# Two-layer encoder on one core: convolution taps spread over the attention, half of their products on VectorE, GpSimd held until the first exponential, and softmax sums inverted before they are turned

## The chip, the cores and the metric

The kernel runs on one core of a Trainium2 chip. The metric is the device time of one execution in microseconds (us), median of several; lower is better. The engines are PE (TensorE, matrix products and transposes), DVE (VectorE), ACT (ScalarE), POOL (GpSimd) and SP (SyncE, which here only issues transfers). POOL also issues transfers, among them all that add into their destination.

## The reference

Two layers of latent attention beside a convolution module, then a gated feed-forward block with a short convolution, on 1024 tokens of width 1024. Cut to what matters here:

```python
for l in range(DEPTH):                       # 2
    h = _rmsnorm(x, g_mix[l]); p = h @ w_in[l]
    ...                                      # q, k, v of 8 heads from low-rank latents
    sc = q_nope @ k_nope.T + q_rope @ k_rope.T          # 1024 x 1024 per head
    y_attn = softmax(sc * scale) @ v
    a, gt = split(p[..., o3:]); u = a * sigmoid(gt)
    u = _dwconv(u, w_dw_conv[l], b_dw_conv[l])          # 31 taps, 512 channels, depthwise
    u = silu(_layernorm(u, g_conv_ln[l], b_conv_ln[l]))
    x = x + concatenate([y_attn, u]) @ w_o[l]
    ...                                      # gated feed-forward block, 2 x 2816 wide
return _rmsnorm(x, g_final)
```

## The kernel before

Everything lies with its channels on the 128 partitions and the 1024 tokens along the row, so the 512 convolution channels are four blocks `u[0]` to `u[3]` (in traces `gate`) with running sums `conv[0]` to `conv[3]`. Products are made in float32 with split operands (names ending in h and l). On PE, DVE, ACT and POOL the program's order is the order written by hand; the transfers of SP are ordered by the framework.

A layer has three stages: `project` (input projections, the near taps of the convolution on DVE), `attention`, and `feed` (output projection, normalizations, feed-forward block). In the profiled execution the attention of layer 0 lies about from 198 to 410 us and that of layer 1 from 1320 to 1530 us.

**The attention's steps.** `attention` walks over 64 pairs of a head and a tile of 128 queries. Step n holds, in this order: for odd n the product of probabilities and values of an earlier pair of tiles (`values`, `o`, line 1565), the transposes of tile n (`turn`, `t`, line 1539) with two copies out of PSUM into `pt` (ACT line 1541, DVE line 1542), the scores of tile n+2 (`s`, line 1516) with their row maximum on DVE (`mx`, line 1518), an exponential on ACT (`p`, line 1526), and last whatever stands in `agenda[n]`, a list of pieces of other work by step. A `values` reads both copies of two tiles, so a late `pt` on either engine stops PE. Two heads share a tile `yt`: `gather` adds the halves of a product into it.

**Row sums.** The exponential leaves row sums as columns `sums` (128 queries x 8 tiles). After a head's last `gather`, `sums` turns them on PE (`sr`, 8 x 128 in PSUM), inverts them on DVE (`rs`, line 1594), writes them to memory and reads them back spread over 64 partitions (`rb`). For every second head POOL multiplies `yt` by `rb` (line 1598) `Y_DELAY` steps later, and later still ACT casts the product (`ys_..h`, line 197) and POOL takes the difference (`ys_..l`, line 199). The last two heads use another way (`inverse`, `spread`).

**Late taps.** The taps that are left after `project` (`away`) are made during the attention by `tap_late`: a product of the shifted block and one column into `late` (line 1723, on POOL or DVE), and then the addition into `conv[j]`, for block 0 on POOL (line 1727), for the other blocks by an adding transfer that POOL issues (line 1729). Two adding transfers into the same block follow each other: the second is issued when the first has landed. The taps of the four blocks take turns, and the step of each comes from running costs (`LATE_COST`, `SIDE_TIME`); block 3 has 15 late taps, block 2 has 11, blocks 0 and 1 have 12 (11 in layer 1). A tap whose product is on DVE has it at the head of an agenda of an even step (steps 4 and 6 of each eight), and its transfer in the next step.

**The end of the attention.** From step 50 on POOL casts weights of the output projection (`wo`, line 850), ACT makes their second part (line 178) and POOL completes them by an adding transfer (line 179). At steps 60 to 62 `conv_total` adds the four blocks into `lns` on POOL (line 1735), and after step 64 `conv_split` casts it on ACT (line 1739) and takes the rest on DVE (line 1740).

Of the kernel before, what the change touches and what calls it, by code (L numbers as in the profile page):

```python
# [9 lines left out]
F32 = mybir.dt.float32  # L10
# [45 lines left out]
SECTION = {"kr": 7.3, "k": 2.72, "u": 4.08, "n": 4.08, "v": 2.72}  # L56
TAP = 1.28
FFN_BANKS = (2, 4)
SIDE_TIME = 57
TOTAL_TIME = 60  # L60
Y_DELAY = 5
Y_LAST = 4
WO_AT = 50
ROWS = (3, 4)
ROW_AT = {0: (6,), 1: (7,)}
# [1 line left out]
MANUAL = [E.PE, E.DVE, E.Activation, E.Pool]  # L67
LATE_COST = {"pool": 2.3, "both": 3.8, "vector": 0.9}
LATE_ADDED = 0
NEAR_TAPS = (12, 14, 16, 14)  # L70
NEAR_ORDER = (0, 1, 2, 3)
FAR_TOGETHER = 3
# [42 lines left out]
class Encoder:  # L115
# [125 lines left out]
    def turned(self, acc, name, parts, bank):  # L241
        out = []
        for s in parts:
            ps = bank(name + "t")
            for b in range(0, s.stop - s.start, 128):
                self.nc.tensor.transpose(ps[:, b:b + 128], acc[:, s.start + b:s.start + b + 128], self.ident)
            out.append(ps[:, 0:s.stop - s.start])
        return out
# [267 lines left out]
    def project(self, l, carry):  # L516
# [54 lines left out]
        def glu(j):  # L571
# [6 lines left out]
            todo = [t for t in range(KC) if t != PAD]  # L578
            taps.extend((j, t) for t in todo[:NEAR_TAPS[j]])
            taps.sort(key=lambda e: NEAR_ORDER.index(e[0]))  # L580
            away[j] = todo[NEAR_TAPS[j]:]
            far_at[j] = 0.0
# [250 lines left out]
    def layer(self, l, carry):  # L833
        with self.psum(f"mix{l}", ([f"w{i}" for i in range(3)], 1), 2):
            mixed = self.project(l, carry)
        with self.psum(f"attn{l}", 2, 2):
            casts, ready = {}, {}
            cast = lambda ms: [casts.update({m: self.wo_cast(l, m, 1)}) for m in ms]
            ahead = {WO_AT: lambda: cast(range(4)), WO_AT + 6: lambda: cast((4, 5)), 62: lambda: cast((6, 7))}
            for m, when in enumerate((55, 59, 60, 62)):  # L840
                ahead[when] = lambda m=m, f=ahead.get(when, lambda: None): (ready.update({(1, m): self.complete(*casts.pop(m))}), f())
            begun = {"x": {}, "po": {}}
            conv, ys = mixed[1], self.attention(l, *mixed, ahead, ready, begun)
        with self.psum(f"ffn{l}", 0, ([f"d{i}" for i in range(8)], 1)):
            return self.feed(l, conv, ys, ready, casts, begun["x"])()
# [43 lines left out]
    def wo_steps(self, l, conv, ys, w, casts, x, steps, put):  # L889
        nc, a, par = self.nc, self.a, self.par[l]  # L890
        left, right = HALVES
        casts, ps, acc, sq, rf, us = {(1, m): e for m, e in casts.items()}, {}, {}, {}, {}, []
# [11 lines left out]
        def turn(part, m):  # L904
            w[part, m] = self.complete(*casts.pop((part, m)))

        put(-3, 0, load_x)
        put(1, 6, self.last_pair)
        for m in range(4, 8):
            put(-1, 3, lambda m=m: turn(1, m))  # L910
        for m in range(8):
            put(m // 4, 5, lambda m=m: cast(0, m))
# [575 lines left out]
    def attention(self, l, u, conv, away, spill, keys, kvs, loaded, ahead, wo, begun):  # L1488
        nc = self.nc
# [3 lines left out]
        state, v = {}, []  # L1493

        def rows(tt):
            (kv, wv), ts = kvs, slice(tt * 128, (tt + 1) * 128)
            ps = self.bank(f"pv{l}_{tt}")
            for k in range(2):
                for s, (i, j) in enumerate(((0, 0), (0, 1), (1, 0))):
                    nc.tensor.matmul(ps, kv[k][i][:, ts], wv[j][:, k * 512:(k + 1) * 512],  # L1500
                                     start=(k == 0 and s == 0), stop=(k == 1 and s == 2))
            if tt % 2 == 0:
                v.append(self.blk(f"v{l}_{tt}", F32, (128, 2, 512)))
            (nc.vector.tensor_copy if tt % 2 else nc.scalar.copy)(out=v[tt // 2][:, tt % 2], in_=ps)
# [69 lines left out]
        def gather(h, gg, main, aux, n):  # L1574
            st = state[h]
            y, rb, po = st["y"], st["rb"], st["po"]
            qs = HALVES[gg]
            nc.scalar.copy(out=y[main, qs], in_=po[aux, :])
            nc.vector.tensor_tensor(out=y[main, qs], in0=po[main, :], in1=y[main, qs], op=ALU.add)
            if h < HEADS - 2:  # L1580
                if gg:
                    agenda[n + 1].append(lambda: sums(h, main, st, y, rb))
            elif n > total:
                divide(y[main, qs], main, h, gg)
            else:
                agenda[n + 1].append(lambda: divide(y[main, qs], main, h, gg))
                if h == last:
                    agenda[n + 1].append(lambda: finish(last, y, 0))

        def sums(h, main, st, y, rb):  # L1590
            pr = self.bank(f"sr{l}_{h}", (8, 128))
            nc.tensor.transpose(pr, st["sums"], self.ident)
            rs = self.cp.tile([8, 128], F32, name=f"rs{l}_{h}", tag="rs", bufs=2)
            nc.vector.reciprocal(out=rs, in_=pr)
            nc.sync.dma_start(out=sd[h].rearrange("(a b) -> a b", a=8), in_=rs)
            nc.sync.dma_start(out=rb[main, :], in_=sd[h:h + 1].partition_broadcast(64))
            if h % 2:
                agenda[h * 8 + 10 + Y_DELAY].append(lambda: nc.gpsimd.tensor_tensor(out=y, in0=y, in1=rb, op=ALU.mult))
                agenda[h * 8 + 10 + Y_DELAY + (Y_DELAY if h < 5 else Y_LAST)].append(
                    lambda: ys.append(self.split(y, f"ys{l}_{h}", on_pool=True)))  # L1600
# [29 lines left out]
        ys, inv, po = [], {}, begun["po"]  # L1630
        total = HEADS * 8
        agenda = defaultdict(list)
        late = [(j, away[j][i]) for i in range(max(map(len, away.values()))) for j in range(4) if i < len(away[j])]
        kinds = ["both" if j == LATE_ADDED else "vector" if i % 4 == 2 and i < len(late) - 6 else "pool" for i, (j, _) in enumerate(late)]
        costs, taken = [LATE_COST[kind] for kind in kinds], set()
        for i, (j, t) in enumerate(late):
            n, steps = int(SIDE_TIME * sum(costs[:i]) / sum(costs)), self.tap_late(l, j, t, u[j], conv[j], kinds[i])
            if kinds[i] == "vector":
                while n % 8 not in (4, 6) or n in taken:
                    n += 1  # L1640
                taken.add(n)
                agenda[n].insert(0, lambda steps=steps: next(steps))
                n += 1
                agenda[n].append(lambda steps=steps: next(steps, None))
            else:
                agenda[n].append(lambda steps=steps: (next(steps), next(steps, None)))
        for when, f in ahead.items():
            agenda[when].append(f)
        last = HEADS - 1
# [5 lines left out]
        self.last_pair = lambda: finish(last, state_y(), 1)  # L1655
        for i in range(1, 4):
            agenda[TOTAL_TIME + i - 1].append(lambda i=i: self.conv_total(l, conv, i))
        agenda[total].append(lambda: self.conv_split(l))
        for n in range(-2, total + 1):
            if n % 2 and n > 2:  # L1660
                values((n - 3) // 2, n)
# [8 lines left out]
            if n + 2 < total:  # L1670
                h, qt = divmod(n + 2, 8)
# [197 lines left out]
```

## Time and profile before

| | us |
|---|---|
| median of 3 runs | 2262.45 |
| the runs | 2262.25, 2262.45, 2269.5 |
| profiled execution, its own time | 2264.65 |
| span of the profiled execution, first to last instruction | 2262.9 |
| PE busy | 2231.8 |
| DVE busy | 1670.9 |
| ACT busy | 1233.4 |
| POOL busy | 729.8 |

Busy time says how long an engine had an instruction under way; PE is busy for 99% of the span, so what matters is the little time in which it waits, and the time in which its clock is lowered (the column PEclk of a table of stretches, 1.00 is the full clock). Rows of the timeline give the start in us, the duration, the engine, the line, the operation, output and inputs; in brackets the idle time of the engine before, and what ended it.

### The profile page before, as it was taken

The numbers are of one execution on the slowest core, as the hardware profiler recorded it, in microseconds if no ns is written. First come the engines' busy times: TensorE is split into PE (matmuls) and PEld (weight loads), VectorE is DVE, ScalarE is ACT, GpSimd is POOL, SyncE is SP. The second block draws the span as 40 slices with busy tenths as digits, with TensorE's granted clock in tenths as the row PEclk, the third lists the DMA queues.
The fourth block names the chain that finished last, engine by engine and source line by source line (L and its number), as shares of the span: only waits on it lengthen the run. The fifth ranks groups of instructions, "written<-read, shape, count | busy, mean of one in ns | idle before, by whom it ended". The sixth has DMA issues, their size and how long they took to land. (4 is left out here: it accounts for less than half of the span.)

```text
span 2262.9 us, 34450 instructions
## 1 busy us (share of the span) xinstructions
PE 2231.8 (99%) x12746; PEld 1790.5 (79%) x12746; DVE 1670.9 (74%) x2200; ACT 1233.4 (55%) x1885; POOL 729.8 (32%) x808
## 2 busy tenths in 40 slices
PE   9999999999999999999999999989999999999998
PEld 7887666787888888888888876667888888888887
DVE  6997877668877776776559778866787777768665
ACT  5444777446655555544533557764475555555444
POOL 1222676432333333001412235762323333320032
PEclk9999999999999999999999999999999999999999
DMA  6889998855899998935968999987669999988356
GB/s 187 164 176 275 188 205 180 205 168 122 216 279 299 274 301 204 336 103 142 211 136 167 194 270 198 191 182 188 162 141 235 277 299 277 298 205 308 103 127 167
DMA packets 201161, 472.85 MB, mean 209 GB/s; under 512 B 28353, under 2 KB 35617, under 8 KB 200993
## 3 DMA queue, kind: packets, MB, share of 16 engines
q0 software_dynamic: 102704, 220.91, 48.6%
q1 hardware_dynamic: 98000, 249.35, 33.3%
q8 instruction: 100, 1.64, 0.3%
q14 instruction: 69, 0.56, 0.1%
q10 hardware_dynamic: 288, 0.39, 0.0%
HBM read 306.14 MB, written 80.40 MB: 171 GB/s over the span
## 5 line engine op out<-in xcount | busy, mean ns | idle before, releaser
L1076 PE MATMUL p<-b,w 128*128 128x512 f32 x3552 | 808.0, 389 | 1.2 <-ACT zv L1087 1.1
L1076 PEld LDWEIGHTS p<-b,w 128*128 128x128 f32 x3552 | 665.8, 188 | 142.8 <-ACT zv L1087 2.2
L1264 PE MATMUL pd<-ab,wd 128*128 128x512 f32 (+1 forms) x1920 | 422.3, 381 | 0.0
L1264 PEld LDWEIGHTS pd<-ab,wd 128*128 128x128 f32 x1920 | 350.7, 188 | 69.5 <-DVE ab L1454 0.4
L179 POOL DMA_DIRECT2D w<-wu x96 | 84.2, 877 | 359.5 <-ACT w L178 323.0
L1518 DVE TENSOR_REDUCE mx<-s 128x1 f32<-128x1024 f32 x128 | 156.2, 1220 | 39.0 <-PE s L1516 31.2
L1526 ACT ACTIVATE p<-s,mx 128x1024 f32<-128x1024 f32 x128 | 143.0, 1117 | 60.0 <-DVE mx L1518 58.3
L1466 DVE SCALAR_TENSOR_TENSOR o<-zg,par,o 128x1023 f32<-128x1023 f32 x88 | 112.8, 1284 | 75.4 <-ACT o L1460 74.0
L179 POOL DMA_DIRECT2D w<-in_w_up x116 | 100.4, 866 | 201.2 <-ACT w L178 181.6
L1710 DVE SCALAR_TENSOR_TENSOR conv<-gate,par,conv 128x1009 f32<-128x1009 f32 (+7 forms) x112 | 142.3, 1274 | 3.6 <-ACT conv L575 1.0
L1565 PE MATMUL o<-pt,v 128*64 128x256 f32 x1024 | 128.1, 388 | 14.1 <-ACT pt L1541 9.4
L178 ACT ACTIVATE w<-w 128x512 fp32r<-128x512 f32 x212 | 133.5, 630 | 3.1
L1025 DVE TENSOR_TENSOR zg<-p,zg 128x512 f32<-128x512 f32 x88 | 60.6, 690 | 99.7 <-PE p L1076 92.9
L1452 ACT CAST ab<-ac 128x512 fp32r<-128x512 f32 x130 | 80.1, 617 | 98.5 <-DVE ac L1199 96.0
L850 POOL DMA_DIRECT2D wd<-in_w_down x44 | 32.6, 745 | 309.5 <-PE pd L1264 309.4
L1542 DVE COPY pt<-t 128x512 f32<-128x512 f32 x128 | 87.8, 686 | 56.5 <-PE t L1539 49.9
L1466 DVE SCALAR_TENSOR_TENSOR v<-zv,par,v 128x1023 f32<-128x1023 f32 x88 | 112.5, 1280 | 10.5 <-ACT v L1460 10.4
L1565 PEld LDWEIGHTS o<-pt,v 128*64 128x64 f32 x1024 | 67.8, 137 | 65.6 <-issue 19.7
L1452 ACT CAST w<-wu 128x512 fp32r<-128x512 f32 x84 | 51.9, 620 | 122.6 <-DVE wu L1025 122.6
L1723 POOL TENSOR_SCALAR late<-gate,par 128x1013 f32<-128x1013 f32 (+14 forms) x77 | 109.4, 1421 | 12.3 <-PE pn L215 12.3
L1043 ACT CAST w<-wu 128x512 fp32r<-128x512 f32 x96 | 58.9, 614 | 94.5 <-DVE wu L1025 91.0
L1539 PEld LDWEIGHTS t<-ident,p 64*128 64x128 f32 x2048 | 77.6, 139 | 40.7 <-issue 27.4
(2140 smaller groups left out, 4384.6 us busy)
## 6 DMA issues: line engine op xcount, KB each, us to landing
w<-in_w_up POOLq DMA_DIRECT2D x232, 256.0 KB, 7.4
wu<-in_w_up SPq DMA_DIRECT2D x88, 512.0 KB, 5.6
w<-wu POOLq DMA_DIRECT2D x96, 256.0 KB, 5.9
sd<-in_w_down SPq DMA_DIRECT2D x44, 512.0 KB, 9.9
ws<-sd SPq DMA_DIRECT2D x44, 512.0 KB, 6.8
wd<-in_w_down POOLq DMA_DIRECT2D x88, 256.0 KB, 5.3
act<-v SPq DMA_DIRECT2D x36, 512.0 KB, 4.9
ac<-act SPq DMA_DIRECT2D x72, 256.0 KB, 6.0
```

The source lines that it names most:

```text
L178: self.nc.scalar.activation(out=lo, in_=hi.bitcast(F32), func=AF.Copy, scale=-1.0)
L179: self.nc.gpsimd.dma_start(out=lo, in_=src, accum_op=ALU.add)
L1076: nc.tensor.matmul(ps, w[p][:, k * 128:(k + 1) * 128], b[:, q], start=(i in (1, 5, 2) and k == 0 and t == 0), stop=(k == 3 and t == 2), sk ...
L1264: nc.tensor.matmul(ps[t, m][:, cs], w[i, j][p][:, m * 128:(m + 1) * 128], b[:, q, cs], start=(i in (1, 5, 2) and j == 0 and s == 0), stop= ...
L1452: nc.scalar.copy(out=t[:, 0], in_=src)
L1466: self.nc.vector.scalar_tensor_tensor(out=o[:, a:b], in0=z[:, at + a:at + b], scalar=self.par[l][:, tap:tap + 1], in1=o[:, a:b], op0=ALU.m ...
L1518: nc.vector.tensor_reduce(out=mx, in_=ps, op=ALU.max, axis=AX.X, negate=True)
L1526: nc.scalar.activation(out=p, in_=ps, func=AF.Exp, bias=mx, accum_out=st["sums"][:, qt:qt + 1])
L1542: nc.vector.tensor_copy(out=pt[:, :, :, 1, :], in_=tp[1])
L1565: nc.tensor.matmul(po[ROW_TILES[i % 2], cs], v[k // 2][:, k % 2, h * 64:h * 64 + 64], pt[:, i, :], start=k < 2, stop=k > 5)
L1710: self.nc.vector.scalar_tensor_tensor(out=y[:, lo:hi], in0=u[:, lo + s:hi + s], scalar=self.tap(l, j, t), in1=y[:, lo:hi], op0=ALU.mult, o ...
L1723: eng.tensor_scalar(out=p[:, lo:hi], in0=u[:, lo + s:hi + s], scalar1=self.tap(l, j, t), scalar2=1.0, op0=ALU.mult, op1=ALU.mult)
```

## The change

- The late taps of each block are spread evenly over the steps from 2 to 53 (`LATE_FROM`, `SIDE_TIME`), so that all four blocks end together; before they took turns until a block had none left.
- The products of blocks 2 and 3 (`LATE_VECTOR`) go to DVE, one at the head of the agenda of nearly every even step; where no even step is free, POOL keeps it. Products on DVE: 50 instead of 21. Products on POOL: 48 instead of 77.
- `agenda[-1]` holds a one-column copy on POOL that reads the first row sums, so that POOL's late taps begin after the first exponential.
- `sums` is split: the columns are inverted first on DVE (`ri`, 128 x 8), and one step later `turned` turns the inverted columns and copies them out (`rs`, 8 x 128) where the inversion was.
- The multiplication by `rb` comes 4 steps after the turn instead of 5, the cast after it 4 (5 for head 5); `conv_total` moves from steps 60 to 62 to steps 58 to 60, `conv_split` from after step 64 to after step 63; the second parts of two more `wo` tiles move from `feed` to steps 63 and 64.
- The value rows 2 and 3 at the start use the PSUM tiles `t0` and `t1` instead of the two rotating banks.

```diff
-SIDE_TIME = 57
-TOTAL_TIME = 60
-Y_DELAY = 5
-Y_LAST = 4
+SIDE_TIME = 53
+TOTAL_TIME = 58
+Y_DELAY = 4
+Y_LAST = 5
...
+LATE_VECTOR = (2, 3)
+LATE_FROM = 2
...
-            for m, when in enumerate((55, 59, 60, 62)):
+            for m, when in enumerate((55, 59, 60, 62, 63, 64)):
...
-            ps = self.bank(f"pv{l}_{tt}")
+            ps = self.bank(f"pv{l}_{tt}") if tt not in (2, 3) else self.pp.tile([128, 512], F32, name=f"pv{l}_{tt}", tag=f"t{tt % 2}", bufs=1)
...
-                    agenda[n + 1].append(lambda: sums(h, main, st, y, rb))
+                    sums(h, main, st, y, rb)
...
         def sums(h, main, st, y, rb):
+            rc = self.cp.tile([128, 8], F32, name=f"ri{l}_{h}", tag="ri", bufs=2)
+            nc.vector.reciprocal(out=rc, in_=st["sums"])
+            agenda[8 * h + 10].append(lambda: turned(h, main, rc, rb, y))
+
+        def turned(h, main, rc, rb, y):
             pr = self.bank(f"sr{l}_{h}", (8, 128))
-            nc.tensor.transpose(pr, st["sums"], self.ident)
+            nc.tensor.transpose(pr, rc, self.ident)
             rs = self.cp.tile([8, 128], F32, name=f"rs{l}_{h}", tag="rs", bufs=2)
-            nc.vector.reciprocal(out=rs, in_=pr)
+            nc.vector.tensor_copy(out=rs, in_=pr)
...
-        late = [(j, away[j][i]) for i in range(max(map(len, away.values()))) for j in range(4) if i < len(away[j])]
-        kinds = ["both" if j == LATE_ADDED else "vector" if i % 4 == 2 and i < len(late) - 6 else "pool" for i, (j, _) in enumerate(late)]
+        late = sorted(((i + 0.5) / len(away[j]), j, t) for j in range(4) for i, t in enumerate(away[j]))
+        kinds = ["both" if j == LATE_ADDED else "vector" if j in LATE_VECTOR else "pool" for _, j, _ in late]
...
+        for i, (_, j, t) in enumerate(late):
+            n, kind = LATE_FROM + int((SIDE_TIME - LATE_FROM) * sum(costs[:i]) / sum(costs)), kinds[i]
+            if kind == "vector":
+                m = next((m for m in range(n + n % 2, n + 5, 2) if m not in taken and m <= SIDE_TIME), None)
+                kind = "pool" if m is None else kind
+            steps = self.tap_late(l, j, t, u[j], conv[j], kind)
+            if kind == "vector":
+                taken.add(m)
+                agenda[m].insert(0, lambda steps=steps: next(steps))
+                agenda[m + 1].append(lambda steps=steps: next(steps, None))
...
+        agenda[-1].append(lambda: nc.gpsimd.tensor_copy(out=self.cp.tile([128, 1], F32, name=f"begun{l}"), in_=state[0]["sums"][:, 0:1]))
...
-        agenda[total].append(lambda: self.conv_split(l))
+        agenda[total - 1].append(lambda: self.conv_split(l))
```

What stands where on the engines, in layer 0 (names of tiles carry running numbers at their end; `late_3_30` is tap 30 of block 3).

POOL at the start of the attention, before:

```order
L179 DMA wv0l<-in_w_v 128x1024
L1723 ISA
L1723 TENSOR_SCALAR late_0_19_1710<-gate_0_407,par_63 128x1020
L1727 TENSOR_TENSOR conv_0_466<-conv_0_466,late_0_19_1710 128x1020
L1723 TENSOR_SCALAR late_1_19_1757<-gate_1_468,par_63 128x1020
L1729 DMA conv_1_530<-late_1_19_1757 128x1020
L1723 TENSOR_SCALAR late_3_16_1843<-gate_3_777,par_63 128x1023
L1729 DMA conv_3_845<-late_3_16_1843 128x1023
```

The same place now:

```order
L181 DMA wv0l<-in_w_v 128x1024
L1655 COPY begun_1686<-sums_0_1628 128x1
L1732 ISA
L1732 TENSOR_SCALAR late_0_19_1794<-gate_0_407,par_63 128x1020
L1736 TENSOR_TENSOR conv_0_466<-conv_0_466,late_0_19_1794 128x1020
L1738 DMA conv_3_845<-late_3_16_1792 128x1023
L1732 TENSOR_SCALAR late_1_19_1881<-gate_1_468,par_63 128x1020
L1738 DMA conv_1_530<-late_1_19_1881 128x1020
```

The copy `begun` stands ahead of all late taps, and the product of tap 16 of block 3 is gone from POOL (DVE makes it); its transfer is left.

POOL near the end of the attention, from the weights' casts to the multiplication of heads 4 and 5, before:

```order
L850 DMA wo_13_4051<-in_w_o 128x512
L1723 TENSOR_SCALAR late_1_30_4106<-gate_1_468,par_63 128x1009
L1729 DMA conv_1_530<-late_1_30_4106 128x1009
L1723 TENSOR_SCALAR late_3_27_4148<-gate_3_777,par_63 128x1012
L1729 DMA conv_3_845<-late_3_27_4148 128x1012
L1729 DMA conv_2_708<-late_2_30_4146 128x1009
L1723 TENSOR_SCALAR late_3_28_4198<-gate_3_777,par_63 128x1011
L1729 DMA conv_3_845<-late_3_28_4198 128x1011
L1723 TENSOR_SCALAR late_3_29_4245<-gate_3_777,par_63 128x1010
L1729 DMA conv_3_845<-late_3_29_4245 128x1010
L1723 TENSOR_SCALAR late_3_30_4294<-gate_3_777,par_63 128x1009
L1729 DMA conv_3_845<-late_3_30_4294 128x1009
```

and the rows from the same cast on now:

```order
L852 DMA wo_13_4073<-in_w_o 128x512
L1738 DMA conv_3_845<-late_3_29_4065 128x1010
L1732 TENSOR_SCALAR late_1_30_4129<-gate_1_468,par_63 128x1009
L1738 DMA conv_1_530<-late_1_30_4129 128x1009
L1732 TENSOR_SCALAR late_3_30_4171<-gate_3_777,par_63 128x1009
L1738 DMA conv_3_845<-late_3_30_4171 128x1009
L1738 DMA conv_2_708<-late_2_30_4169 128x1009
L1605 TENSOR_TENSOR yt_4_3315<-yt_4_3315,rb_4_3316 128x1024
L181 DMA wo_10_4067<-in_w_o 128x512
```

Before, four taps of block 3 follow each other between the cast and the multiplication of `yt`; now two do, and the multiplication follows directly.

ACT at the end of the attention, before:

```order
L1541 COPY pt_7_30_4645<-t_7_300_4627 128x8x64
L1541 COPY pt_7_31_4681<-t_7_310_4663 128x8x64
L1739 CAST lns0h<-lns_4527 128x1024
L1578 COPY yt_6_4059<-o_7_1_4618 64x512
L178 ACTIVATE wo_14_4336<-wo_14_4336 128x512
```

and now:

```order
L1543 COPY pt_7_30_4659<-t_7_300_4641 128x8x64
L180 ACTIVATE wo_14_4350<-wo_14_4350 128x512
L1748 CAST lns0h<-lns_4443 128x1024
L1543 COPY pt_7_31_4701<-t_7_310_4683 128x8x64
L180 ACTIVATE wo_15_4352<-wo_15_4352 128x512
L1580 COPY yt_6_4081<-o_7_1_4632 64x512
```

The cast of `lns`, which waits for POOL, has moved ahead of the last copy of probabilities; on DVE the subtraction that follows it (line 1749 now) stands ahead of that tile's other copy in the same way.

More of the change, by code (lines that the diff above doesn't have):

```diff
@@ L908, in wo_steps @@
         put(1, 6, self.last_pair)
-        for m in range(4, 8):
+        for _, m in sorted(casts):
             put(-1, 3, lambda m=m: turn(1, m))
@@ L1632, in attention @@
         agenda = defaultdict(list)
-        late = [(j, away[j][i]) for i in range(max(map(len, away.values()))) for j in range(4) if i < len(away[j])]
-        kinds = ["both" if j == LATE_ADDED else "vector" if i % 4 == 2 and i < len(late) - 6 else "pool" for i, (j, _) in enumerate(late)]
+        late = sorted(((i + 0.5) / len(away[j]), j, t) for j in range(4) for i, t in enumerate(away[j]))
+        kinds = ["both" if j == LATE_ADDED else "vector" if j in LATE_VECTOR else "pool" for _, j, _ in late]
         costs, taken = [LATE_COST[kind] for kind in kinds], set()
[L1636 to L1644, printed above, removed]
+        for i, (_, j, t) in enumerate(late):
[8 more added lines that the diff above has]
+                agenda[m + 1].append(lambda steps=steps: next(steps, None))
             else:
                 agenda[n].append(lambda steps=steps: (next(steps), next(steps, None)))
+        agenda[-1].append(lambda: nc.gpsimd.tensor_copy(out=self.cp.tile([128, 1], F32, name=f"begun{l}"), in_=state[0]["sums"][:, 0:1]))
         for when, f in ahead.items():
```

## The prediction

> **What bounds the kernel now.** I read the page first, then the stretches around the attention, then who PE waited for, then the timeline at each wait.
>
> ```profile
> span 2262.9 us, 34450 instructions
> ```
>
> PE is busy in nearly all of it, and the change alters none of PE's work. So it can only win back time in which PE waits or runs at a lowered clock, and can only lose by new waits. The waits by releaser (us in total, times, longest):
>
> ```profile
> PE o L1565 <- ACT pt L1541: 9.4, 2, 5.8
> PE t L1539 <- DVE pt L1542: 2.5, 3, 1.4
> PE pv L1500 <- DVE v L1504: 2.0, 1, 2.0
> ```
>
> and the stretches of the three long ones, each with the stretch behind it, then the steady part of each layer's attention (columns: stretch, its length, busy time of PE, PEld, DVE, ACT, POOL, clock):
>
> ```profile
> 204.20:206.30 2.10, 0.12 (x3) 0.08 (x1) 2.10 (x3) 0.61 (x1) 1.80 (x3) 1.00 1.01 402
> 206.50:210.10 3.60, 3.60 (x12) 2.40 (x13) 1.49 (x2) 1.21 (x2) 3.22 (x4) 0.53 1.05 298
> 389.60:393.30 3.70, 0.08 (x4) 0.07 (x4) 0.36 (x2) 1.65 (x3) 3.70 (x5) 1.00 1.01 172
> 394.30:397.80 3.50, 3.50 (x30) 2.57 (x29) 0.86 (x2) 2.66 (x5) 3.50 (x3) 0.51 0.81 159
> 1506.50:1512.40 5.90, 0.07 (x4) 0.01 (x2) 0.42 (x2) 1.59 (x3) 5.78 (x7) 0.84 0.77 130
> 1512.40:1517.40 5.00, 5.00 (x34) 3.10 (x34) 0.69 (x1) 3.82 (x7) 5.00 (x4) 0.51 0.89 175
> 216.00:390.00 174.00, 170.25 (x2055) 117.66 (x2054) 137.66 (x158) 126.51 (x208) 110.20 (x91) 1.00 0.93 201
> 1334.00:1507.00 173.00, 170.17 (x2056) 117.62 (x2054) 137.10 (x157) 126.46 (x208) 103.23 (x86) 1.00 0.93 203
> ```
>
> After each long wait PE is busy all through, but at half its clock. The price of a wait is thus the idle time plus (1 - clock) times the stretch behind it: 3.60 x 0.47 = 1.7, 3.50 x 0.49 = 1.7, 5.00 x 0.49 = 2.45 us.
>
> **The end waits.** POOL's timeline at the end of layer 1's attention, with the rows of ACT and PE that follow from it, and PE's in layer 0:
>
> ```profile
> 1490.67 0.90 POOL L1729 DMA_DIRECT2D conv<-late  x1 [6.56 <-DMA conv<-late]
> 1496.48 0.89 POOL L1729 DMA_DIRECT2D conv<-late  x1 [3.74 <-issue]
> 1501.52 0.88 POOL L1729 DMA_DIRECT2D conv<-late  x1 [2.98 <-issue]
> 1506.62 0.89 POOL L1729 DMA_DIRECT2D conv<-late  x1 [3.06 <-DMA conv<-late]
> 1507.76 3.02 POOL L1598 TENSOR_TENSOR yt<-yt,rb 128x1024 f32<-128x1024 f32 x1
> 1510.81 1.04 ACT L197 CAST ys_5h<-yt 128x1024 fp32r<-128x1024 f32 x1 [7.03 <-POOL yt L1598]
> 1512.39 1.98 PE L1565 MATMUL o<-pt,v 128*64 128x256 f32 x8 [5.83 <-ACT pt L1541]
> 393.23 1.08 PE L1565 MATMUL o<-pt,v 128*64 128x256 f32 x8 [3.62 <-ACT pt L1541]
> ```
>
> The last taps of block 3 alone are left, each transfer waits for the landing of the one before (every 5 to 6 us), and the multiplication of `yt` stands behind them on POOL. ACT, whose program puts the cast `ys_5h` ahead of the next `pt`, stands still, and PE with it. Removed: 5.83 + 2.45 = 8.3 us in layer 1, 3.62 + 1.7 = 5.3 in layer 0, together **-13.6**.
>
> Will it go in full? Durations for POOL:
>
> ```profile
> L1723 POOL TENSOR_SCALAR late<-gate,par x77: 1102/1432/3145, 197.8 to 1502.1; 128x1009 f32<-128x1009 f32 x7, 128x1019 f32<-128x1019 f32 x6, 128x1018 f32<-128x1018 f32 x6, 128x1017 f32<-128x1017 f32 x6
> L1727 POOL TENSOR_TENSOR conv<-conv,late x23: 2334/2366/2862, 199.0 to 1467.9; 128x1019 f32<-128x1019 f32 x2, 128x1018 f32<-128x1018 f32 x2, 128x1017 f32<-128x1017 f32 x2, 128x1016 f32<-128x1016 f32 x2
> L1729 POOL DMA_DIRECT2D conv<-late x75: 847/885/1002, 204.8 to 1506.6; - x75
>   DVE late L1723: 59.0, 11
> DMA to landing us min/median/max: 4.5/7.0/11.6
> L1539 PE MATMUL t<-ident,p x1024: 213/222/366, 1334.8 to 1525.3; 64*128 64x64 f32 x171
> L1598 POOL TENSOR_TENSOR yt<-yt,rb x6: 2385/2719/3036, 284.1 to 1507.8; 128x1024 f32<-128x1024 f32 x6
> ```
>
> The transposes of 64 steps take 190.5 us from first to last; less the 8.3 above and over 63 that is 2.9 us a step. Now POOL's queue from step 51 on holds: transfer of tap 29 of block 3 (0.9), its landing (7.0, in which POOL makes the other product), two transfers (1.8), the multiplication (2.7): 12.4 us, 4.3 steps, so done near step 55 or 56. ACT wants it in step 59; three steps or 9 us are spare, against a POOL that came 7 us late. So in full; bounds: nothing gained (POOL as late as now) and 13.6.
>
> **The start.**
>
> ```profile
> 199.29 6.28 DVE L719 SCALAR_TENSOR_TENSOR qn<-qn,qns 128x1024 fp32r<-128x1024 f32 x3
> 201.35 3.15 POOL L1723 TENSOR_SCALAR late<-gate,par 128x1020 f32<-128x1020 f32 x1
> 205.49 0.68 DVE L1504 COPY v<-pv 128x512 f32<-128x512 f32 x1
> 206.22 0.50 PE L1500 MATMUL pv<-wv0h,kvs_0h 128*128 128x512 f32 x1 [1.98 <-DVE v L1504]
> 1317.81 2.36 DVE L719 SCALAR_TENSOR_TENSOR qn<-qn,qns 128x1024 fp32r<-128x1024 f32 x2 [0.72 <-ACT qns L713]
> 1322.96 0.50 PE L1500 MATMUL pv<-wv1h,kvs_0h 128*128 128x512 f32 x1 [0.35 <-ACT v L1504]
> ```
>
> Three subtractions on DVE take 6.28 us while POOL makes its first taps; with POOL idle two take 2.36, so three would take 3.5. POOL's own product takes 3.15 instead of 1.43. Held until the first exponential, POOL leaves DVE 2.7 us earlier, and with rows 2 and 3 in other PSUM tiles PE does not ask for that copy at all. Next late there is the first maximum, behind the same subtractions and so earlier too; PE has rows 3 to 5 and the second scores to do meanwhile. I take 1.98 + 1.7 and 0.35: **-4.0** (bounds 0 and -4.0). The hold costs POOL some 9 us of head start; it has 29 products fewer, 29 x 1.43 = 41 us over both layers, so nothing comes of it. [...]
>
> **The added work on DVE.**
>
> ```profile
> L1723 DVE TENSOR_SCALAR late<-gate,par x21: 727/749/2919, 228.7 to 1466.7; 128x1019 f32<-128x1019 f32 x2, 128x1018 f32<-128x1018 f32 x2, 128x1017 f32<-128x1017 f32 x2, 128x1016 f32<-128x1016 f32 x2
> L1723 DVE TENSOR_SCALAR late<-gate,par 128x1019 f32<-128x1019 f32 (+10 forms) x21 | 21.6, 1028 | 0.3
> L1594 DVE RECIPROCAL rs<-sr x12: 931/933/935, 245.8 to 1478.5; 8x128 f32<-8x128 f32 x12
> L1604 DVE RECIPROCAL rc<-sums x8: 167/169/179, 367.3 to 1520.5; 128x4 f32<-128x4 f32 x8
> ```
>
> 29 products more at 0.75 are 21.7 us. The inversion of 128 values along a row (0.93) becomes one of 8 (between the 0.17 of four and twice that, I take 0.2) and a copy (between 0.17 and the 0.68 of the 128x512 copy, I take 0.25): 12 x 0.48 = 5.8 us saved. Net 8 us a layer: DVE goes from 137.7 of 174 (79%) to 146 (84%). Each product lies between a maximum and the next copy, where 174 - 137.7 = 36 us are idle over some 30 pairs of steps, 1.2 us a pair. I take +0.5 us a layer, **+1.0** (bounds 0 and 3, for steps that also gather `yt`).
>
> What the median hides is the collision:
>
> ```profile
> 279.75 2.86 POOL L1727 TENSOR_TENSOR conv<-conv,late 128x1015 f32<-128x1015 f32 x1
> 280.23 2.92 DVE L1723 TENSOR_SCALAR late<-gate,par 128x1015 f32<-128x1015 f32 x1
> 283.81 0.65 PE L1539 MATMUL t<-ident,p 64*128 64x64 f32 x14 [1.40 <-DVE pt L1542]
> ```
>
> A tap on DVE that meets POOL computing ends only after POOL does: 2.17 us over its 0.75, of which PE pays 1.40, or 0.65 us each. How often? Between two taps on DVE, mostly two steps or 5.8 us apart, POOL has one transfer and either product and addition (0.9 + 1.43 + 2.37 = 4.7) or product and transfer (3.2). It finishes first and waits, as it does now (59.0 us in 11 waits for DVE), and a waiting POOL collides with nothing. Where a multiplication or subtraction of `yt` (2.7) comes between, 7.4 us don't fit and the next two taps collide: four places a layer, 16 taps, at some 0.6 us over = 10 us. Now the same excess is 21.6 (all 21 together) - 21 x 0.75 = 5.9. At 0.65 the difference would be 2.7; DVE has less slack to take it up, so I take **+4** (bounds: all gone, 2.5 us won; every tap hit, below).
>
> **Edits costed at nothing.** The later queue order of SP (keys ahead of queries of the next heads) is covered by eight steps until use. `begun` is one column. POOL's multiplication waits for `rb`, now four steps (11.6 us) after the turn; three spare steps cover it. The cast of `lns` ahead of the last `pt` on ACT, and its remainder on DVE: after `ys_5h` in step 59 POOL has two transfers, two additions and a subtraction, 2 x 0.9 + 3 x 2.4 to 2.7, some 10 us, against 4 steps or 11.6; PE has nine products in between. If that cover goes, PE waits what POOL is late (bounds 0 and 3 us a layer).
>
> **Sum.** -13.6 - 4.0 + 1.0 + 4.0 = -12.6 us. The profiled execution took 2264.65 (1.75 around its span) and would take 2252; the median stood 2.2 lower at 2262.45, so **2250**.
>
> **Rivals.**
> - *The end wait stays in another form.* POOL is still late, behind landings of up to 11.6 us, or the cast of `lns` now holds the `pt` copies. For it: three transfers into conv blocks and four `wo` casts still stand ahead of the multiplication. Against it: the 9 us spare. Then -4.0 + 5.0 = +1, 2263.5 with the whole wait, and 2257 with half of it.
> - *The taps on DVE collide everywhere (slower).* POOL starts late, never gets ahead, and each of the 50 taps meets a product or an addition, with a mean rest of 1.2 us. Price: 50 x 1.2 x 0.65 = 39, less the 2.5 of now, so -17.6 + 1 + 36.5 = +20, 2282. It turns to slower by 7 us once (17.6 + 7 - 1 + 2.5) / (1.2 x 0.65) = 33 of 50 taps collide. For it: the 2.92 row. Against it: the median of 0.749 says that most taps miss POOL now, while it has more work. [...]
> - *The change costs nothing at all:* no collision is left, -17.6 - 2.5 = 2242.
>
> **How the numbers follow.** Forecast family (both waits gone, some collisions) 0.74; end wait in another form 0.14; collisions 0.08; nothing lost 0.04. About 0.3% or 6.8 us is what a measurement of this kernel tells from no change. Faster takes the first, the last: 0.78, with a little from half the wait lost to same 0.14, slower 0.08. The range is 2242 (no cost) to 2260 (most of the end wait left).
>
> **What would show it.** PE's waits for ACT `pt` fall from 9.4 to under 1 us; the clock in layer 0's start and both ends is 1.00; DVE's three subtractions take about 3.5 us; POOL's multiplication for head 5 ends several us before ACT's cast of it begins. DVE's 50 products keep a median of 0.75, and PE's waits for DVE `pt` grow to some 5 us. Wrong would be: a mean of the products above 1.5 us, or a new wait of PE at the last copies.

## The result, and the profile after

The changed kernel takes 2251.68 us (median of five, 2249.87 to 2253.84) against 2263.29 for the kernel before on the same chip (2262.25 to 2269.5). The ratio is 0.994, with a 95% interval of 0.9924 to 0.9957: faster by 0.4 to 0.8%. The forecast was 2250.0. The profiled execution's span fell by 13.0 us:

```profile
span 2249.9 us, 34444 instructions
```

Who PE waited for (us in total, times, longest), the five longest items of the list:

```profile
PE sr L1599 <- DVE ri L1594: 6.0, 12, 0.6
PE t L1541 <- DVE pt L1544: 4.2, 4, 1.4
PE o L1567 <- DVE yt L1581: 1.6, 2, 0.8
PE o L1567 <- DVE pt L1544: 1.2, 6, 0.2
PE pv L1502 <- DMA wv0l<-in_w_v: 1.1, 1, 1.1
```

The waits for ACT `pt` (9.4 before) and for DVE `v` (2.0) are gone from the list. At its head stands a wait that did not exist: the transpose `sr` waits in each of the 12 turns for the inverted columns `ri`. The same stretches as before (length, busy time of PE, PEld, DVE, ACT, POOL, then the clock): the start, and the ends of layers 1 and 0.

```profile
204.20:206.30 2.10, 2.10 (x15) 1.47 (x12) 0.96 (x1) 1.62 (x2) 0.00 (x0) 1.00 1.02 408
206.50:210.10 3.60, 3.60 (x20) 2.47 (x19) 1.98 (x3) 1.46 (x3) 2.08 (x3) 1.00 1.02 405
1506.80:1513.60 6.80, 5.98 (x66) 4.23 (x62) 4.89 (x8) 4.89 (x8) 5.40 (x6) 1.00 0.86 241
386.00:398.00 12.00, 11.19 (x127) 7.64 (x123) 8.38 (x12) 9.00 (x16) 10.70 (x8) 1.00 0.65 161
```

PE works through all of them at clock 1.00, but for one wait of 0.8 us at each end, which stood there before too. POOL's last transfer and its multiplication of `yt` for heads 4 and 5, with ACT's cast of the product, in layer 1 and then in layer 0:

```profile
1485.15 1.79 POOL L1738 DMA_DIRECT2D conv<-late  x2 [7.39 <-DMA conv<-late]
1486.30 3.05 POOL L1605 TENSOR_TENSOR yt<-yt,rb 128x1024 f32<-128x1024 f32 x1
1500.09 1.03 ACT L199 CAST ys_5h<-yt 128x1024 fp32r<-128x1024 f32 x1
370.88 2.60 POOL L1605 TENSOR_TENSOR yt<-yt,rb 128x1024 f32<-128x1024 f32 x1
384.53 1.04 ACT L199 CAST ys_5h<-yt 128x1024 fp32r<-128x1024 f32 x1
```

The multiplication ends at 1489.35 and 373.48, 11 us before its cast; before, the cast stood waiting for it. The start, DVE's three subtractions and the copy that holds POOL:

```profile
199.62 3.49 DVE L721 SCALAR_TENSOR_TENSOR qn<-qn,qns 128x1024 fp32r<-128x1024 f32 x3
207.86 0.18 POOL L1655 COPY begun<-sums 128x1 f32<-128x1 f32 x1 [15.15 <-ACT p L1528]
```

And the two prices of the new order on DVE: first the inversion, which stands behind the addition into `yt` while PE is ready for its transpose, then the longest product, which meets POOL's subtraction and keeps the next copy from PE.

```profile
1398.35 0.67 DVE L1581 TENSOR_TENSOR yt<-o,yt 64x512 f32<-64x512 f32 x1
1398.95 0.18 DVE L1594 RECIPROCAL ri<-sums 128x8 f32<-128x8 f32 x1
1399.19 0.27 PE L1599 MATMUL sr<-ident,ri 128*8 128x128 f32 x1 [0.38 <-DVE ri L1594]
1400.69 2.46 POOL L201 TENSOR_TENSOR ys_1l<-yt,ys_1h 128x1024 fp32r<-128x1024 f32 x1 [0.36 <-ACT ys_1h L199]
1400.75 2.95 DVE L1732 TENSOR_SCALAR late<-gate,par 128x1017 f32<-128x1017 f32 x1
1404.54 0.65 PE L1541 MATMUL t<-ident,p 64*128 64x64 f32 x14 [1.29 <-DVE pt L1544]
```

### The profile page after: what moved, and what is told of

Same layout as the page of the kernel before. It is cut to its first block, busy times and chain, and to the rows that moved or that the text cites. A ratio compares the mean times of both kernels' runs of the same rounds, so it can differ in the third digit from the quotient of the medians.

```text
span 2249.9 us, 34444 instructions
## 1 busy us (share of the span) xinstructions
PE 2225.7 (99%) x12746; PEld 1790.3 (80%) x12746; DVE 1687.8 (75%) x2241; ACT 1235.2 (55%) x1885; POOL 693.4 (31%) x781
## 5 line engine op out<-in xcount | busy, mean ns | idle before, releaser
L1738 POOL DMA_DIRECT2D conv<-late x75 | 68.3, 924 | 123.6 <-DVE late L1732 54.3
```

## The experiments

All start from the changed kernel. Times are medians in us with the lowest and highest run; the ratio is to the kernel before on the same chip, whose median lay between 2263.3 and 2265.3 in all sets.

| kernel | us | ratio, 95% interval |
|---|---|---|
| changed kernel | 2251.68 (2249.87 to 2253.84) | 0.9940 (0.9924 to 0.9957) |
| e_turns: taps by turns again | 2265.44 (2262.36 to 2267.02) | 1.0007 (0.9998 to 1.0016) |
| e_old_taps: order, kinds and steps of the taps as before | 2261.34 (2259.11 to 2263.5) | 0.9990 (0.9978 to 1.0001) |
| e_old_ends: old steps of the ends | 2250.72 (2249.61 to 2252.39) | 0.9937 (0.9923 to 0.9951) |
| e_no_hold: POOL not held | 2252.34 (2249.14 to 2255.07) | 0.9949 (0.9930 to 0.9969) |
| e_old_banks: rows 2 and 3 in rotating banks | 2252.71 (2249.09 to 2257.67) | 0.9957 (0.9938 to 0.9976) |
| e_old_start: both of these | 2253.59 (2252.84 to 2256.02) | 0.9957 (0.9943 to 0.9970) |
| e_row_inverse: row inverted behind the transpose | 2256.96 (2254.45 to 2260.03) | 0.9966 (0.9953 to 0.9978) |
| e_ri_early: columns inverted two steps earlier | 2245.55 (2241.73 to 2250.5) | 0.9919 (0.9892 to 0.9946) |
| e_ri_odd: and POOL's work on `yt` in odd steps | 2249.24 (2244.89 to 2250.68) | 0.9926 (0.9912 to 0.9939) |
| e_pool_products: every product on POOL | 2246.67 (2245.79 to 2248.85) | 0.9920 (0.9906 to 0.9934) |
| c_pool_ri: e_pool_products and e_ri_early | 2242.52 (2242.06 to 2242.85) | 0.9906 (0.9891 to 0.9921) |
| c_pool_ri_50: and taps only up to step 50 | 2251.22 (2249.86 to 2255.76) | 0.9950 (0.9937 to 0.9962) |

**The order of the taps (e_turns).**

```diff
-        late = sorted(((i + 0.5) / len(away[j]), j, t) for j in range(4) for i, t in enumerate(away[j]))
+        late = [(i, j, away[j][i]) for i in range(max(map(len, away.values()))) for j in range(4) if i < len(away[j])]
```

> The changed kernel with one line put back: the late taps take turns until a block has none left; products, rule of steps and their end at 53 stay as changed. Theory A (the order is what removes the end waits: three or four taps of block 3 follow each other at 5 to 7 us each): PE waits at the ends of both layers, for ACT pt, or for DVE pt behind the totals, 3 to 8 us in all with half clock: 2255 to 2262. Theory B (the earlier end at step 53 is enough in any order): no wait above 1.4 us after step 55: 2250 to 2253.

Measured: 13.8 us slower than the changed kernel, above theory A's range. Two of PE's waits, then POOL and PE at the end of layer 1, the stretch behind the wait, and last POOL and ACT at the end of layer 0:

```profile
PE t L1541 <- DVE pt L1544: 8.0, 7, 1.3
PE o L1567 <- ACT pt L1543: 7.0, 1, 7.0
1496.58 0.88 POOL L1738 DMA_DIRECT2D conv<-late  x1 [7.69 <-DMA conv<-late]
1501.64 0.87 POOL L1738 DMA_DIRECT2D conv<-late  x1 [3.01 <-DMA conv<-late]
1506.73 0.85 POOL L1738 DMA_DIRECT2D conv<-late  x1 [4.22 <-DMA conv<-late]
1507.29 2.65 POOL L1605 TENSOR_TENSOR yt<-yt,rb 128x1024 f32<-128x1024 f32 x1
1511.56 0.70 PE L1567 MATMUL o<-pt,v 128*64 128x256 f32 x2 [7.01 <-ACT pt L1543]
1511.60:1515.10 3.50, 3.50 (x28) 2.27 (x30) 0.45 (x1) 3.11 (x6) 3.50 (x4) 0.52 0.99 203
382.73 2.72 POOL L1605 TENSOR_TENSOR yt<-yt,rb 128x1024 f32<-128x1024 f32 x1
385.70 1.04 ACT L199 CAST ys_5h<-yt 128x1024 fp32r<-128x1024 f32 x1
```

In layer 1 this is the picture of before: transfers of one block that wait for each other's landing, the multiplication behind them, ACT and PE behind it, then half clock. In layer 0 POOL is just in time: the multiplication ends at 385.45, 0.25 us ahead of its cast, and PE does not wait for it. So this execution gives back one of the two end waits, 7.0 + 1.7 = 8.7 us, and 3.8 us of waits for DVE `pt` on top (8.0 instead of 4.2; in this order 45 products are left on DVE). Its span is 11.2 us above that of the changed kernel; it was shorter than most of the ten, and no trace shows whether layer 0 waits in the longer ones. Ending the taps at step 53 instead of 57 was not enough in layer 1. By the time, nothing of the change's gain is left without this one line of order.

**All of the taps as before (e_old_taps).** The order, the kinds and the rule of steps of the diff above are put back together (the loop with the rule of the steps is left out here):

```diff
-        late = sorted(((i + 0.5) / len(away[j]), j, t) for j in range(4) for i, t in enumerate(away[j]))
-        kinds = ["both" if j == LATE_ADDED else "vector" if j in LATE_VECTOR else "pool" for _, j, _ in late]
+        late = [(j, away[j][i]) for i in range(max(map(len, away.values()))) for j in range(4) if i < len(away[j])]
+        kinds = ["both" if j == LATE_ADDED else "vector" if i % 4 == 2 and i < len(late) - 6 else "pool" for i, (j, _) in enumerate(late)]
...
-SIDE_TIME = 53
+SIDE_TIME = 57
...
```

> The changed kernel with the late taps alone put back: turns until a block has none left, 21 products on DVE, steps up to 57. All else is new (hold, PSUM tiles, inverted columns, earlier multiplication and totals). Theory (the serial landings of block 3 hold POOL up): both end waits come back, PE waits for ACT pt 8 to 10 us in 2 pieces with a stretch at half clock behind each, +13.6; the waits for DVE pt fall from 4.2 to about 2.5, -1.7: 2251.7 + 12 = 2263 to 2265. Rival 1 (the earlier multiplication and totals removed the end waits): within 3 us of 2251.7 and no wait for ACT pt. Rival 2 (half and half): one of the two layers waits, 2256 to 2259.

Measured: 9.7 us slower than the changed kernel, below the theory's range, and the wait is in another place. Its waits, and DVE at the end of layer 1:

```profile
PE t L1541 <- DVE pt L1544: 8.4, 5, 3.6
PE o L1567 <- ACT pt L1543: 0.5, 1, 0.5
1512.86 7.16 DVE L1635 SCALAR_TENSOR_TENSOR ys_7l<-yt,ys_7h 128x512 fp32r<-128x512 f32 x1 [0.74 <-issue]
1516.06 3.41 POOL L1743 TENSOR_TENSOR lns<-lns,conv 128x1024 f32<-128x1024 f32 x1
```

The earlier multiplication did remove the wait for ACT `pt` (0.5 left), as rival 1 had it. But POOL's subtraction `ys_5l` and late totals then ran beside DVE's subtraction `ys_7l`, which took 7.16 us, and PE waited 3.56 us for the copy behind it. In layer 0 the same subtraction took 4.93 us and PE waited 2.86. Behind the wait of layer 0 the clock was 0.50 over 3.40 us, behind that of layer 1 it was 0.50 over 3.70 us and then 0.83 over 3.50, which costs 4.1 us; with the two waits that is 10.6 us against the 13.6 of the end waits before. A late POOL cost most of that in the new place too; the steps only chose where.

**The steps of the ends (e_old_ends).**

```diff
-TOTAL_TIME = 58
-Y_DELAY = 4
-Y_LAST = 5
+TOTAL_TIME = 60
+Y_DELAY = 5
+Y_LAST = 4
...
-        agenda[total - 1].append(lambda: self.conv_split(l))
+        agenda[total].append(lambda: self.conv_split(l))
```

> The changed kernel with the late taps spread as it has them, but with the old steps of the ends: multiplication by rb 5 steps after the turn, casts 5 and 4 steps later, the totals of the convolution from step 60, their split after step 64. Theory A (with the taps spread POOL is early enough for either set of steps): no wait for ACT pt above 1 us, 2251 to 2254. Theory B (the spread and the earlier steps are both needed, as the old taps with the new steps moved the wait to the totals): PE waits 1 to 3 us a layer for pt or for ys_5 or the split, with half clock behind those near 2: 2255 to 2261.

Measured: 2250.72, just below the range of theory A, and no wait for ACT `pt`. With the taps spread, these steps are worth nothing that can be measured.

**The start (e_no_hold, e_old_banks, e_old_start).** The first drops the line with `begun`, the second puts `self.bank(f"pv{l}_{tt}")` back for rows 2 and 3, the third does both.

> The changed kernel without the one-column copy that holds POOL until the first exponential; rows 2 and 3 keep their own PSUM tiles. Theory A (the tiles alone keep PE from asking for the late copy): DVE's three subtractions take 6.2 us again, but PE has no wait of 1.98 us at about 206 and no half clock: 2251 to 2253. Theory B (PE runs into the late maximum or copy elsewhere): a wait of 1.5 to 2.5 us in layer 0 with 3.6 us at half clock behind it, +3.2 to +4.2: 2255 to 2256.

> The changed kernel with rows 2 and 3 of the values back in the two rotating PSUM banks; the hold of POOL stays. Theory A (the hold alone suffices, DVE is done 2.7 us earlier): no wait above 0.5 us at 203 to 207, 2251 to 2253. Theory B (the bank is asked for before the copy in any case): the wait of PE for DVE v stays at 0.5 to 2.0 us, with half clock if it is near 2: +0.5 to +3.7, 2252 to 2255.5.

> The changed kernel without both edits of the start: POOL isn't held, and rows 2 and 3 use the rotating banks (each alone left no wait). Theory A (either is enough, both together make the start term): PE waits 1.5 to 2 us for DVE v at about 206 in layer 0, with a stretch at half clock, and 0.35 in layer 1: 2251.7 + 3 to 4 = 2254.5 to 2256. Theory B (another edit, such as the order of SP's queue or what DVE has there, removes it): no wait above 0.5 us between 202 and 210: 2251 to 2253.

Measured: none of the three differs from the changed kernel by more than the intervals allow, and none has the wait of 1.98 us. With both edits undone, DVE, PE and POOL at the start:

```profile
199.61 4.33 DVE L721 SCALAR_TENSOR_TENSOR qn<-qn,qns 128x1024 fp32r<-128x1024 f32 x3
199.79 3.07 POOL L1731 TENSOR_SCALAR late<-gate,par 128x1020 f32<-128x1020 f32 x1 [7.08 <-DVE qn L713]
202.95 3.23 POOL L1735 TENSOR_TENSOR conv<-conv,late 128x1020 f32<-128x1020 f32 x1
204.59 0.50 PE L1502 MATMUL pv<-wv0h,kvs_0h 128*128 128x512 f32 x1 [0.23 <-DVE v L1506]
```

Theory A of the third kernel fell: neither edit is needed against the long wait of layer 0. The short one of layer 1 is another matter: with the rotating banks, in e_old_banks and e_old_start, PE waits 0.38 and 0.36 us for ACT `v` there, as the 0.35 before; with the other tiles it does not. POOL's first tap begins at 199.79 here and at 197.77 before, where an addition and a second product followed under the same subtractions (6.28 us instead of 4.33; in e_no_hold too they take 4.33, and not the 6.2 expected). What is left of the change there is that taps begin at step 2 (`LATE_FROM`). That this is the cause is argued from these rows; it was not run alone.

**The inversion (e_ri_early, e_row_inverse).** The first inverts the columns in step 8h+8:

```diff
-            rc = self.cp.tile([128, 8], F32, name=f"ri{l}_{h}", tag="ri", bufs=2)
-            nc.vector.reciprocal(out=rc, in_=st["sums"])
...
+        for h in range(HEADS - 2):
+            agenda[8 * h + 8].append(lambda h=h: invert(h))
...
```

> The changed kernel with the inversion of the columns two steps earlier (step 8h+8, where the sums are complete, instead of behind the last addition of the product in step 8h+9); the transpose stays in step 8h+10. Theory (PE waits for the inversion only because it stands behind that addition on DVE): the 12 waits of the transpose for ri, 6.0 us, are gone; -4.4 to -6: 2245.7 to 2247.3. Rival (PE only waits a little later, for the addition into yt behind the same copies, as it did six times before, 1.6 us, or the PSUM bank of the transpose is not free): 0 to -2, 2249.7 to 2251.7, with new waits for DVE yt of some 4 to 6 us.

The second turns `sums` and inverts the row, as before:

```diff
-            rc = self.cp.tile([128, 8], F32, name=f"ri{l}_{h}", tag="ri", bufs=2)
-            nc.vector.reciprocal(out=rc, in_=st["sums"])
...
-            nc.vector.tensor_copy(out=rs, in_=pr)
+            nc.vector.reciprocal(out=rs, in_=pr)
```

> The changed kernel with the old inversion alone: the sums are turned first and the row of 8 x 128 is inverted (0.93 us on DVE instead of 0.19 and 0.27). Theory A (the wait of the transpose for the inverted columns costs more than the shorter inversion saves): the 12 waits, 6.0 us, go, six waits of 0.2 for DVE yt come back, -4.4 with DVE's 5.6 us more mostly beside other work, waits for DVE pt up by 0 to 2: 2247 to 2250. Theory B (with 25 products a layer on DVE its time is scarce, 12 x 0.47 = 5.6 us all on the path): 2251 to 2254, waits for DVE pt of 8 us or more.

Measured: the earlier inversion wins 6.1 us between medians, though its runs spread over 8.8, the longest lies among those of the changed kernel, and the intervals of the two ratios overlap; its list of waits has no `sr` any more. Its profiled execution, the slowest of its four, has waits for DVE `pt` of 7.2 instead of 4.2 and behind one of them a clock of 0.66 over 3.40 us (1.2 us), so part of the gain can come back through collisions. The row costs 5.3 us, against theory A; theory B had the place right and its size too small. DVE in that kernel, and PE's longest item of waits:

```profile
1401.01 2.95 DVE L1730 TENSOR_SCALAR late<-gate,par 128x1017 f32<-128x1017 f32 x1
1403.88 0.94 DVE L1599 RECIPROCAL rs<-sr 8x128 f32<-8x128 f32 x1
1404.75 0.62 DVE L1544 COPY pt<-t 128x512 f32<-128x512 f32 x1
PE t L1541 <- DVE pt L1544: 8.9, 5, 2.7
```

The inversion stands between a product that collided and the copy for which PE waits; there its 0.94 us counts in full, and it lengthens a wait of 1.3 to one of 2.15, behind which the clock was 0.55 over 3.40 us; behind another of the five waits it was 0.69 (behind others of this length it stayed at 1.00, last section). The two stretches cost 2.6 us of the 4.9 by which this span is longer, while the waits of its attention are in sum no longer than the changed kernel's; so about half of the loss is the clock in these stretches alone. By the medians the inverted columns are worth 5.3 us with their wait, and 11.4 without it (2256.96 against 2245.55; the second is less certain, as the runs of e_ri_early spread so far).

**The products on DVE (e_pool_products, e_ri_odd).**

```diff
-LATE_VECTOR = (2, 3)
+LATE_VECTOR = ()
```

> The changed kernel with the taps spread, but every product on POOL (98 instead of 48) and none on DVE. Theory A (POOL becomes late: 50 products more at 1.43 are 36 us a layer of about 155 in steps 2 to 53): PE waits for ACT pt behind the casts of yt, 5 to 9 us a layer with half clock: 2262 to 2272. Theory B (POOL keeps up, since it has idle time between landings): the waits behind collisions of DVE's products, 4.2 us, are gone and nothing comes: 2247 to 2249.

Measured: 2246.67, 5.0 us faster than the changed kernel by the medians, just below theory B; no run of one reaches those of the other, though the intervals of the two ratios just overlap. Its waits have no `t` for DVE `pt`; POOL late costs 1.4 us once:

```profile
PE sr L1599 <- DVE ri L1594: 6.1, 12, 0.6
PE o L1567 <- ACT pt L1543: 1.4, 1, 1.4
```

So moving half of the products to DVE costs about 5 us here and is not needed for the spread. The other way to avoid collisions moves POOL's multiplications and subtractions of heads 1 and 3 by one step, with the earlier inversion:

```diff
+                odd = 1 if h < 5 else 0
-                agenda[h * 8 + 10 + Y_DELAY].append(lambda: nc.gpsimd.tensor_tensor(out=y, in0=y, in1=rb, op=ALU.mult))
-                agenda[h * 8 + 10 + Y_DELAY + (Y_DELAY if h < 5 else Y_LAST)].append(
+                agenda[h * 8 + 10 + Y_DELAY + odd].append(lambda: nc.gpsimd.tensor_tensor(out=y, in0=y, in1=rb, op=ALU.mult))
+                agenda[h * 8 + 10 + Y_DELAY + odd + (Y_DELAY if h < 5 else Y_LAST)].append(
```

> The changed kernel with the columns inverted two steps earlier, and POOL's multiplications and subtractions of yt for heads 1 and 3 one step later, in odd steps, where DVE has no product. Theory A (the long collisions stand where the subtraction falls in an even step, 26 and 42): the products above 2 us are halved at least, waits for DVE pt fall from 7.2 (inversion earlier alone) to 2 to 4: 2241 to 2243. Theory B (POOL runs by landings and not by steps, so that the collisions only move): waits for DVE pt stay 5 to 8 us, 2244 to 2247, as with the earlier inversion alone.

Measured: 2249.24, above both ranges, though by the ratios not told apart from the earlier inversion alone. The products with over 2 us are 7 instead of 5, the waits for DVE `pt` 6.2:

```profile
PE t L1541 <- DVE pt L1544: 6.2, 8, 1.3
```

Theory A fell: the collisions moved and did not go. That they moved because POOL runs by landings and not by steps is theory B's reading; no run tests it alone.

**Both finds together (c_pool_ri, c_pool_ri_50).** The diffs of e_ri_early and e_pool_products in one kernel; then with `SIDE_TIME = 50`.

> The changed kernel with both finds together: the taps spread with every product on POOL, and the columns inverted two steps earlier. Theory A (the two costs are separate: 12 waits for ri, 6.0 us, and the collisions): waits for ri 0, six waits of 0.13 for DVE yt, waits for DVE pt under 1 us, the wait of 1.4 us for ACT pt in layer 1 stays: 2246.7 - 5.2 = 2241.5, range 2240 to 2243. Theory B (the 0.27 copy and the next copies come late behind the inversion anyway, so a part returns as waits for DVE pt of 2 to 4 us): 2244 to 2246.

> The kernel of the row above, with the taps spread up to step 50 instead of 53. Theory A (ACT's wait in layer 1 comes from the weights' cast, whose transfers stand behind late taps on POOL): the wait of 1.4 us goes, 2239 to 2241. Theory B (POOL's taps follow each other by landings, 7.0 us median, so that an earlier due step ends nothing earlier): the wait stays within 0.5 us, 2241 to 2243.

Measured: 2242.52, as theory A had it. Its slowest run is 7.0 us under the fastest of the changed kernel, and 2.9 under the fastest of e_pool_products; so the earlier inversion is worth some 4 us here (4.2 by the medians), against runs that lie close together. What is left of waits in its attention is 0.8 at both ends, 0.9 for ACT `pt` once and six of 0.2:

```profile
PE o L1567 <- DVE yt L1581: 1.6, 2, 0.8
PE o L1567 <- DVE pt L1544: 1.2, 6, 0.2
PE o L1567 <- ACT pt L1543: 0.9, 1, 0.9
```

With the taps due three steps earlier, both theories fell: 2251.22, 8.7 us slower. POOL, ACT and PE in layer 1:

```profile
1446.01 0.88 POOL L1743 DMA_DIRECT2D conv<-late  x1 [7.52 <-DMA conv<-late]
1450.42 2.33 POOL L1607 TENSOR_TENSOR yt<-yt,rb 128x1024 f32<-128x1024 f32 x1
1452.78 1.04 ACT L199 CAST ys_3h<-yt 128x1024 fp32r<-128x1024 f32 x1 [8.56 <-POOL yt L1607]
1455.46 0.80 PE L1541 MATMUL t<-ident,p 64*128 64x64 f32 x10 [8.07 <-ACT pt L1543]
```

One more transfer, with a product and an addition of the next taps, stands ahead of the multiplication for heads 2 and 3. The transfer waits 7.5 us for a landing, and the chain of the end waits appears in the middle. The kernel with all products on POOL is fast, but it stands near this edge.

## Why the prediction was right, and where not

The total came out 1.7 us from the median, but two of its terms were wrong by 3.4 and 2.3 us, in opposite directions, and a stage that it left out moved by almost 2; that the sum agrees so well is luck. What carries it is the first term, and that one was right in place and size. The sum by the traces' waits, before to after:

| term | predicted | by the traces |
|---|---|---|
| end waits | -13.6 | -13.6 |
| start | -4.0 | -3.3 |
| added work on DVE | +1.0 | +4.4 |
| collisions | +4.0 | +1.7 |
| feed-forward stages | 0 | -1.8 |
| sum | -12.6 | -12.6, span -13.0 |

- **End waits: right, and shown.** Both waits and their half clocks are gone in full. Putting the order back costs 13.8 us, but that this is so near to 13.6 is chance: the trace of e_turns has one of the two end waits (8.7 us with its half clock) and, beside it, more waits for DVE `pt`. With all of the taps as before (e_old_taps) the loss shows at the ends of both layers, one engine further. The 9 us to spare were 11. As predicted, the multiplication ends well before its cast.
- **Start: right in size, the cause not.** 1.98 us idle, 1.7 of half clock and the 0.35 of layer 1 are gone; the wait for the weights `wv0l` grew from 0.36 to 1.1, but it differs from kernel to kernel (up to 1.2) with nothing changed there. DVE's subtractions take 3.49 us as forecast (3.5). But the two edits to which the term was put down are not needed for its 3.7 us of layer 0; only the 0.35 of layer 1 comes back with the rotating banks.
- **Added work on DVE: the step that failed.** It priced the inverted columns as DVE time alone, 5.8 us saved. Inverting first makes the transpose depend on DVE, behind an addition that ends just then: 12 waits, 6.0 us. Six old waits for `yt` behind the transpose are gone (row below, of before: 3.2, now 1.6), so +4.4, outside the bounds of 0 and 3. The saving was also mis-sized: by e_row_inverse it pays for that wait and for 5.3 us more, an estimate of 4.4 + 5.3 = 9.7 us of the kernel's time from 5.8 us of DVE's.

```profile
PE o L1565 <- DVE yt L1579: 3.2, 8, 0.8
```

- **Collisions: right in kind, the number partly luck, over-priced against before.** DVE's 50 products:

```profile
L1732 DVE TENSOR_SCALAR late<-gate,par x50: 729/745/2947, 220.7 to 1479.9; 128x1019 f32<-128x1019 f32 x4, 128x1018 f32<-128x1018 f32 x4, 128x1017 f32<-128x1017 f32 x4, 128x1016 f32<-128x1016 f32 x4
```

The median is 0.745 as forecast. Fifteen took over 1 us (predicted 16), and their excess is 51.6 - 50 x 0.745 = 14 us (10). The prediction had them as the two products behind each multiplication or subtraction of `yt`. Eight of the fifteen are such; the other seven, one of 2.86 us among them, meet POOL's products and additions of taps elsewhere, and seven of the sixteen places that it named have none. PE paid 4.2 of it, 0.30 us per us instead of the 0.65 taken from one row; the waits for DVE `pt` went from 2.5 to 4.2 (forecast: some 5). Against no products on DVE at all they cost 5.0 us by the medians (e_pool_products); the prediction compared 50 with 21 and never with none.
- **Edits costed at nothing:** right for the later totals and the cast of `lns`; no wait of theirs is in the list, and e_old_ends measures them at nothing. The two more second parts of `wo` tiles in steps 63 and 64 are not in the prediction at all.
- **Rivals.** A different end wait didn't come, but e_old_taps and c_pool_ri_50 show it: there a late POOL was paid for at whatever waited next, with waits of PE of 3.56 and 8.07 us. Collisions everywhere did not come; four products of 50 took over 2 us. A change that costs nothing did not come either: the waits for `ri` and the collisions are both in the list.
- **Feed-forward stages, not in the prediction.** The -1.8 are waits of before, 1.1 us for ACT `zv` and 0.7 for a `wo` transfer. The first comes and goes (0.8 in e_old_ends, 0.3 in e_row_inverse, none in the changed kernel) and belongs to the execution. The second is in the trace of before and in none of the kernels with the change; it can come from the two `wo` pieces that moved out of `feed`, which were not run alone.

## What to carry to other kernels

Where adding transfers into one block wait for each other's landing, spread each block over the whole stage: in layer 1 before, a last run of block 3's transfers, with 3.0 to 6.6 us of idle time ahead of each, held up the multiplication behind them on POOL, then ACT for 7.03 us and PE for 5.83. When an operation is moved ahead of a transpose to make it cheaper, price the new dependency and not only the time saved, and put it where its input is complete, not where the next step happens to stand. Giving a second engine half of the work is worth undoing as a trial once the order is right: here the changed kernel with no product on DVE and the inversion early (c_pool_ri) is 0.94% faster than before instead of 0.6%.

## What the runs showed of the hardware

**The clock after short waits.** After waits of PE of up to 1.53 us in the attention the clock stayed at 1.00. Of ten waits from 1.63 to 2.65 us in all kernels six were followed by a lowered clock (0.54 to 0.70 over the next 3.4 us) and four were not; all six from 2.86 us up were. The stretch behind a wait of 1.71 us (e_no_hold) and behind one of 2.65 us (e_row_inverse), with the clock third from the end:

```profile
338.94:342.34 3.40, 3.40 (x29) 2.39 (x31) 2.35 (x3) 1.70 (x3) 0.88 (x1) 0.62 0.72 136
338.90:342.30 3.40, 3.40 (x41) 2.50 (x41) 3.11 (x4) 1.86 (x4) 0.64 (x1) 1.00 0.76 144
```

So length alone doesn't decide between 1.6 and 2.7 us; what else decides, no run here shows.

**Subtractions beside POOL.** DVE's subtraction of a 128x512 half (`ys_7l`) took 7.16 us while POOL ran a subtraction and totals one after another (e_old_taps); the four such halves of the changed kernel take 0.69 us on average. Three subtractions of 128x1024 at the start took 6.28 us beside an addition and a product of POOL (before), 4.33 beside a product and the start of an addition (e_old_start), and 3.49 with POOL idle (changed kernel).
